# A transformer encoder layer on one core: TensorE's order in the attention written out, with filler in six portions per unit, and residual steps, norm sums, first wave and tail rearranged

## The chip, the cores and the metric

The kernel runs on one core of a Trainium2 chip. A core has five engines with a queue each, all in order: TensorE (PE, matrix products and transposes), VectorE (DVE), ScalarE (ACT), GpSimd (POOL) and SyncE (SP, which here issues the DMAs). An instruction waits in its queue until what it needs is done, and what stands behind it waits too. The metric is the time of one execution in microseconds (us); less is better.

## The reference

One layer over 2048 tokens with 1024 features, all in float32. `mod` holds six vectors made from the conditioning input `c`:

```
mod = silu(c) @ ada_w + ada_b                 # sh1, sc1, g1, sh2, sc2, g2
h = rmsnorm(x, mix_norm_pre) * (1 + sc1) + sh1
q, k, v = split(h @ w_qkv)                    # 16 query heads of 64, 4 key/value heads
logits = q k^T / 8 + bias                     # blocks of 128 queries against 3 x 128 keys
p = softmax([logits, sink])[..., :-1]         # |key - query| <= 128
y = (p v) @ w_o
x = x + g1 * rmsnorm(y, mix_norm_post)
h = rmsnorm(x, ffn_norm_pre) * (1 + sc2) + sh2
y = (silu(a) * b) @ w_out,  a, b = split(h @ w_in)   # 2816 hidden features
x = x + g2 * rmsnorm(y, ffn_norm_post)
```

## The kernel before, in words

Tokens lie in four chunks of 512 columns, features in tiles of 128 partitions. A float32 matrix is split into a high part (rounded, `act.copy`, ScalarE) and a low part (the rest, a subtraction on VectorE or GpSimd); `three` (line 147) multiplies hi x hi, hi x lo and lo x hi, three matmuls of 512 columns. A norm's sum over features is a matmul with ones (`rstd_of`, line 118), as a rule with the sum of squares split in the same way (lines 128 to 132), then a logarithm, an exponential and one Newton step (lines 136 to 141).

Stages, by their place in the profiled execution:

- 0 to 23.5 us: load and norm of chunk 0. 23.5 to 74: the first wave, seven of the twelve q/k/v tiles of chunk 0, with the feature tile k as the outer loop, so that each of eight steps needs one more weight piece (split by ScalarE and GpSimd) and two reductions of the modulation (`ada_reduce`, 128x1024, VectorE).
- to 177: the rest of chunk 0 and chunk 1. `evac` (line 208) splits a finished tile into a buffer `e` (two buffers) and writes it to DRAM (`q_d`, `k_d`, `v_d`).
- 177 to 750: attention in 64 units, one for a chunk c, a group g of four heads with one key/value head, and a query block jb. `scores` (line 421) makes for each of the four heads two matmuls, a VectorE step that adds the bias and finds the maximum (line 437), and an exponential on ScalarE; then a reciprocal and four normalisations on GpSimd (line 445). `values` (line 448), two units later (`LAG`), has for each of three key blocks four transposes, a split of the result (`phi` on ScalarE, `plo` on VectorE) and two products into `o`, then two additions and a DMA to `o_d`. Between the units stands filler: in the first 32 units q/k/v of chunks 2 and 3 (`psq`, 576 matmuls), in the last 32 the output projection of chunks 0 to 2 (`py`, 576 matmuls), whose inputs `ol` are loaded from `o_d` and split, and whose weights `wor` are loaded, split into `wo`, and kept in `wo_d`. A finished projection chunk has steps at its end (`ends`, line 586): norm, residual (three GpSimd operations a tile, lines 507 to 515), norm, `h2`.
- 750 to 821: the projection of chunk 3 (GpSimd's split goes to VectorE there). To 2085: the feed-forward network by a seven-product scheme for 2x2 blocks. To 2164: its last part and the end of the layer; the norms of chunks 2 and 3 (`lo`, `l`) lie inside the feed-forward part.

The program order is written unit by unit (line 652), `fill.pull` giving 18 or 20 filler matmuls after each. A scheduler then orders the instructions of each engine by its own costs and priorities, so the order on an engine is not the program's. `tc.issue_after` holds an instruction until another is placed. SP has one queue, in which loads and writes of all stages stand in turn.

Of the kernel before, what the change touches and what calls it, by code (L numbers as in the profile page):

```python
# [11 lines left out]
F32 = mybir.dt.float32  # L12
# [34 lines left out]
FILL = (18, 20)  # L47
# [7 lines left out]

HOLD = 6
# [17 lines left out]
def encoder_layer(ctx, tc, a):  # L74
    nc = tc.nc
    out = a["out"]
    act, dve, pool, pe, sp = nc.scalar, nc.vector, nc.gpsimd, nc.tensor, nc.sync

# [39 lines left out]
    def rstd_of(alloc, psp, ptag, acc, tag, r=None, direct=False):  # L118
# [5 lines left out]
        if direct or len(sums) > 1:  # L124
            for i, sq in enumerate(sums):
                pe.matmul(ps, f(ones), sq, start=i == 0, stop=i == len(sums) - 1)
        else:
            hi, lo = alloc(f"nhi{tag}")[:, :n].bitcast(F32R), alloc(f"nlo{tag}")[:, :n].bitcast(F32R)
            dve.tensor_copy(hi, acc)
            dve.tensor_tensor(lo, acc, f(hi), ALU.subtract)  # L130
            pe.matmul(ps, ones, hi, start=True, stop=False)
            pe.matmul(ps, ones, lo, start=False, stop=True)
# [7 lines left out]
        dve.tensor_scalar(t, t, -0.5, 1.5, ALU.mult, ALU.add)  # L140
        dve.tensor_tensor(r, r, t, ALU.mult)
# [5 lines left out]
    def three(ps, w, h, first=False, last=False):  # L147

        pe.matmul(ps, w[0], h[0], start=first, stop=False)  # L149
        pe.matmul(ps, w[0], h[1], start=False, stop=False)  # L150
        pe.matmul(ps, w[1], h[0], start=False, stop=last)  # L151
# [55 lines left out]

    def evac(c, n, ps, psp, ptag):

        t = ev.tile([P, 2, CH], F32R, tag="e", name=f"e{c}_{n}")  # L210
# [30 lines left out]
    with ExitStack() as pa:  # L241
        w2 = open_pool(pa, "w2", side="right")
        raws = open_pool(pa, "raws", 5, side="right")
        w1 = open_pool(pa, "w1", side="right")
        psA = open_pool(pa, "psA", 8, space=PSUM)
# [5 lines left out]
        sp.dma_start(gains, a["gains"])  # L251
        act.activation(cb, cb, AF.Silu)
# [3 lines left out]
        def ada_load(t, pl):  # L256
            w = pl.tile([P, D], F32, tag="raw", name=f"ada{t}")
            sp.dma_start(w, a["ada_w"][t])
            return t, w
# [6 lines left out]
        def w_piece(k, i):  # L266
# [3 lines left out]
            t = pl.tile([P, 2, n], F32R, name=f"w{i}_{k}")  # L270
# [21 lines left out]
        for n in NORD[:WAVE]:  # L292
            evac(0, n, pss[n], psA, "mm")
# [3 lines left out]
        ch1.squares()  # L297
# [835 lines left out]
```

## Time and profile before

| what | us |
|---|---|
| runs | 2163.07, 2168.15, 2168.44 (median 2168.15) |
| the profiled execution | 2166.07, of which the span 2164.3 |
| first wave | 23.5 to 74 |
| attention, first half | 184 to 464 |
| attention, second half | 464 to 750 |
| projection of chunk 3 begins | 750 |
| feed-forward | 821 to 2085 |

The page gives busy time of each engine over the span. The view by windows gives the same for stretches, with the mean granted clock of TensorE (PEclk, 1.00 is full speed). The waits tell what an engine's idle time ended with: "s L432 <- DVE nm L437" is a score that waited until a VectorE step of line 437 had freed its buffer. In a timeline a row has start, length, engine, line, operation, out<-in and count; brackets hold the idle time before it and what released it.

### The profile page before, as it was taken

The numbers are of one execution on the slowest core, as the hardware profiler recorded it, in microseconds if no ns is written. First come the engines' busy times: TensorE is split into PE (matmuls) and PEld (weight loads), VectorE is DVE, ScalarE is ACT, GpSimd is POOL, SyncE is SP. The second block draws the span as 40 slices with busy tenths as digits, with TensorE's granted clock in tenths as the row PEclk, the third lists the DMA queues.
The fourth block names the chain that finished last, engine by engine and source line by source line (L and its number), as shares of the span: only waits on it lengthen the run. The fifth ranks groups of instructions, "written<-read, shape, count | busy, mean of one in ns | idle before, by whom it ended". The sixth has DMA issues, their size and how long they took to land. (4 is left out here: it accounts for less than half of the span.)

```text
span 2164.3 us, 28995 instructions
## 1 busy us (share of the span) xinstructions
PE 2055.8 (95%) x9366; PEld 1666.6 (77%) x9366; DVE 1649.8 (76%) x2933; ACT 1076.4 (50%) x2125; POOL 737.5 (34%) x687
## 2 busy tenths in 40 slices
PE   6898999989989989999999999999999999998996
PEld 4786877878867768878887877888888788877886
DVE  7656767665676669876878897767673888999987
ACT  4546666577777746343434342333332844465422
POOL 3404343367778723434344422222221000220030
PEclk8999999999999989999999999999999999999998
DMA  8877665576667695545455764332231644438442
GB/s 279 261 254 253 184 182 175 159 282 233 227 199 245 189 347 206 183 148 162 138 178 194 257 220 142 112 106 94 98 117 54 210 153 138 141 129 280 161 132 103
DMA packets 200516, 396.35 MB, mean 183 GB/s; under 512 B 20091, under 2 KB 62124, under 8 KB 195244
## 3 DMA queue, kind: packets, MB, share of 16 engines
q1 hardware_dynamic: 199788, 393.97, 54.7%
q8 instruction: 74, 1.21, 0.2%
q14 instruction: 78, 0.64, 0.1%
q10 hardware_dynamic: 576, 0.52, 0.1%
HBM read 270.65 MB, written 123.76 MB: 182 GB/s over the span
## 5 line engine op out<-in xcount | busy, mean ns | idle before, releaser
L437 DVE CUSTOM_DVE_ANT_0 pr<-s,bias,nsink 128x384 f32<-128x384 f32 (+1 forms) x256 | 149.3, 596 | 91.5 <-PE s L432 74.3
L149 PE MATMUL pc_i<-ht,ws_i 128*128 128x512 f32 x528 | 207.2, 393 | 2.1 <-DVE b_i L799 1.5
L150 PE MATMUL pc_i<-ht,ws_i 128*128 128x512 f32 x528 | 206.9, 392 | 0.0
L151 PE MATMUL pc_i<-ht,ws_i 128*128 128x512 f32 x528 | 206.9, 392 | 0.0
L439 ACT ACTIVATE pr<-pr,nm 128x385 f32<-128x385 f32 (+1 forms) x256 | 153.8, 603 | 71.3 <-DVE nm L437 64.3
L815 POOL TENSOR_TENSOR p_i<-p_i,u_i 128x512 f32<-128x512 f32 x44 | 71.5, 1625 | 310.7 <-DVE u_i L802 153.6
L445 POOL TENSOR_SCALAR pr<-pr,rs 128x384 f32<-128x384 f32 (+1 forms) x256 | 147.4, 601 | 83.0 <-DVE rs L443 82.9
L946 POOL TENSOR_TENSOR z<-z,z 128x512 f32<-128x512 f32 x32 | 52.5, 1654 | 359.2 <-DVE z L942 342.3
L432 PE MATMUL s<-k,q 128*128 128x384 f32 (+1 forms) x512 | 136.1, 359 | 20.2 <-DVE nm L437 13.6
L149 PE MATMUL pc_i<-hb,wa_i 128*128 128x512 f32 x352 | 139.1, 395 | 2.0 <-DVE u_i L789 2.0
L150 PE MATMUL pc_i<-hb,wa_i 128*128 128x512 f32 x352 | 138.7, 394 | 0.0
L151 PE MATMUL pc_i<-hb,wa_i 128*128 128x512 f32 x352 | 138.7, 394 | 0.0
L155 DVE TENSOR_TENSOR plo<-t,phi 128x512 fp32r<-128x512 f32 x184 | 121.7, 685 | 16.2 <-ACT phi L154 14.7
L154 ACT CAST wa_i<-wiri 128x512 fp32r<-128x512 f32 x132 | 81.8, 620 | 102.2 <-PE pc_i L151 94.7
L154 ACT CAST ws_i<-s_i 128x512 fp32r<-128x512 f32 x132 | 81.6, 618 | 102.5 <-PE pc_i L151 98.7
L432 PEld LDWEIGHTS s<-k,q 128*128 128x128 f32 x512 | 86.6, 193 | 44.9 <-DVE nm L437 27.8
L149 PEld LDWEIGHTS pc_i<-ht,ws_i 128*128 128x128 f32 x528 | 99.3, 188 | 25.5 <-DVE b_i L799 2.2
L151 PEld LDWEIGHTS pc_i<-ht,ws_i 128*128 128x128 f32 x528 | 99.2, 188 | 22.4
L150 PEld LDWEIGHTS pc_i<-ht,ws_i 128*128 128x128 f32 x528 | 99.2, 188 | 22.2
L455 PE MATMUL t<-ident,pr 128*128 128x128 f32 x736 | 113.1, 273 | 3.1 <-POOL pr L445 2.4
L149 PE MATMUL py<-ol,wo 128*128 128x512 f32 x256 | 103.3, 405 | 11.9 <-ACT wo L154 7.4
L155 DVE TENSOR_TENSOR ws_i<-s_i,ws_i 128x512 fp32r<-128x512 f32 x132 | 104.6, 792 | 10.9 <-ACT ws_i L154 10.7
(320 smaller groups left out, 6142.8 us busy)
## 6 DMA issues: line engine op xcount, KB each, us to landing
wiri<-w_in SPq DMA_DIRECT2D x88, 512.0 KB, 4.8
ada<-ada_w SPq DMA_DIRECT2D x40, 512.0 KB, 4.9
wiro<-w_out SPq DMA_DIRECT2D x48, 384.0 KB, 3.9
q_d<-e SPq DMA_DIRECT2D x64, 256.0 KB, 3.9
q<-q_d SPq DMA_DIRECT2D x16, 1024.0 KB, 5.8
wo<-wo_d SPq DMA_DIRECT2D x16, 1024.0 KB, 5.7
g_d_b<-p_i SPq DMA_DIRECT2D x44, 256.0 KB, 4.7
g_d_t<-p_i SPq DMA_DIRECT2D x40, 256.0 KB, 2.0
```

The source lines that it names most:

```text
L149: pe.matmul(ps, w[0], h[0], start=first, stop=False)
L150: pe.matmul(ps, w[0], h[1], start=False, stop=False)
L151: pe.matmul(ps, w[1], h[0], start=False, stop=last)
L154: act.copy(hi, src)
L155: return eng.tensor_tensor(lo, src, f(hi), ALU.subtract).ins
L432: m = pe.matmul(ps[:, :n], q[:, h, jb * P:(jb + 1) * P], kk[:, i, (jb + j0) * P:(jb + j1) * P], start=i == 0, stop=i == 1)
L437: red = dve.tensor_tensor_reduce(pr[:, h, :n], ps[:, :n], bias[g][:, h, j0 * P:j1 * P], -1.0, nsink[:, hh:hh + 1], ALU.add, ALU.min, nm[:, ...
L439: act.activation(pr[:, h, :n + 1], pr[:, h, :n + 1], AF.Exp, bias=nm[:, h:h + 1], scale=-1.0, accum_out=rs[:, h:h + 1])
L445: pool.tensor_scalar(pr[:, h, :n], pr[:, h, :n], rs[:, h:h + 1], 1.0, ALU.mult, ALU.mult)
L455: pe.transpose(pt[:, h * P:(h + 1) * P], pr[:, h, jj * P:(jj + 1) * P], ident)
L815: pool.tensor_tensor(sa, sa, b, ALU.mult)
L946: (pool if (i, x) in ((2, 2), (4, 4), (5, 5), (6, 6)) else dve).tensor_tensor(sums[hf, n2, x], sums[hf, n2, x], sums[hf, n2, y], ALU.add)
```

## The change

1. `FILL` becomes a table with one number per unit; the matmuls of scores, transposes, products and filler are stamped (`inorder`), so TensorE takes them in program order. `scores` and `values` become generators, and a unit is written as: two scores, filler, transposes, one score, filler, transposes, one score, filler, product, transposes, filler, product, filler, product, filler, each filler a sixth of the unit's number.
2. The steps at a projection chunk's end are taken one per unit (`end_step`), two residual tiles each, by turns all on GpSimd and all on VectorE, with two sums; `HOLD` goes; every third weight tile of the projection comes into two separate halves; 66 filler matmuls remain after the last product, where 53 did.
3. Norm sums are no longer split. In the feed-forward part the sums of `lo` and `l` are issued a step later. The Newton step loses an instruction: its factor -0.5 goes into `gains`, on GpSimd.
4. In the first wave the first eight modulation tiles are loaded into the buffers of the second weight part, `evac` has a third buffer (`eva`) for every third tile, and the squares of chunk 1 come after the wave's last evacuation, on VectorE.
5. q, k, v and bias of unit 0 are loaded with high priority, `x` of chunk 3 after them. In the tail, `finish` of the last chunk's first half is spread over n = 4 to 7.

```diff
-FILL = (18, 20)
+FILL = [0, 4, 12, 16] + 16 * [20] + 12 * [19] + [4, 8, 12] + 21 * [17] + 8 * [12]
...
+    def inorder(m):
+        tc.stamp_issue_order_token(m.ins, "attention")
+        return m
...
-        if direct or len(sums) > 1:
-            for i, sq in enumerate(sums):
-                pe.matmul(ps, f(ones), sq, start=i == 0, stop=i == len(sums) - 1)
-        else:
-            hi, lo = alloc(f"nhi{tag}")[:, :n].bitcast(F32R), alloc(f"nlo{tag}")[:, :n].bitcast(F32R)
-            dve.tensor_copy(hi, acc)
-            dve.tensor_tensor(lo, acc, f(hi), ALU.subtract)
-            pe.matmul(ps, ones, hi, start=True, stop=False)
-            pe.matmul(ps, ones, lo, start=False, stop=True)
+        for i, sq in enumerate(sums):
+            pe.matmul(ps, f(ones), sq, start=i == 0, stop=i == len(sums) - 1)
...
-        dve.tensor_scalar(t, t, -0.5, 1.5, ALU.mult, ALU.add)
-        dve.tensor_tensor(r, r, t, ALU.mult)
+        dve.scalar_tensor_tensor(r, t, -3.0, r, ALU.add, ALU.mult)
...
-        t = ev.tile([P, 2, CH], F32R, tag="e", name=f"e{c}_{n}")
+        ev_, nev[0] = (eva if nev[0] % 3 == 2 and c < 2 else ev), nev[0] + 1
+        t = ev_.tile([P, 2, CH], F32R, tag="e", name=f"e{c}_{n}")
...
+        pool.tensor_scalar(gains, gains, -0.5, 1.0, ALU.mult, ALU.mult)
...
-                ada_reduce(*ada_load(8 + k, raws))
-                ada_reduce(*ada_load(k, raws))
+                for t in (8 + k, k):
+                    ada_reduce(*ada_load(t, w2 if k < KT // 2 else raws))
...
-        ch1.squares()
+        with tc.issue_after(ins):
+            ch1.squares((dve, dve))
...
-                dve.tensor_scalar(nsink, nsink, -1.0, None, ALU.mult)
+                pool.tensor_scalar(nsink, nsink, -1.0, 1.0, ALU.mult, ALU.mult)
...
-    def residual(c, k, y, xr, r, acc, alloc, eng=dve):
+    def residual(c, k, y, xr, r, acc, engs=(pool, dve, pool), first=True):
         sp.dma_start(xr, a["xT"][c, :, k, :])
-        pool.tensor_tensor(y, y, r, ALU.mult)
-        eng.tensor_tensor(y, y, xr, ALU.add)
+        engs[0].tensor_tensor(y, y, r, ALU.mult)
+        engs[1].tensor_tensor(y, y, xr, ALU.add)
...
             for k in range(KT):
-                residual(c, k, self.ys[k], yp.tile([P, CH], F32, tag="xr", name=f"xr{c}_{k}", bufs=3), r,
-                         self.acc, rot(yp, "nsq", 4), pool)
-                if k % 4 == 3:
+                residual(c, k, self.ys[k], yp.tile([P, CH], F32, tag="xr", name=f"xr{c}_{k}", bufs=4), r,
+                         accs[k % 2], [(pool, dve)[k % 2]] * 3, False)
+                if k % 2 and k < KT - 1:
                     yield
+            dve.tensor_tensor(accs[0], accs[0], accs[1], ALU.add)
...
+    def end_step():
+        while ending and next(ending[0], ending) is ending:
+            del ending[0]
...
-    load_qkv(0, 0)
-    load_bias(0)
+    with tc.high_priority(offset=400):
+        load_bias(0)
+        first_load = load_qkv(0, 0)
...
-        un.scores()
+        sc = un.scores()
+        vl = units[i - LAG].values() if i >= LAG else iter(())
+        part = FILL[i] / 6
+        next(sc)
+        next(sc)
+        fill.pull(part)
+        next(vl, None)
+        next(sc)
+        fill.pull(part)
+        next(vl, None)
+        next(sc)
...
-        if i >= LAG:
-            units[i - LAG].values()
-            done = i - LAG + 1
-        fill.pull(FILL[i >= half])
+        fill.pull(part)
+        next(vl, None)
+        next(vl, None)
+        fill.pull(part)
+        next(vl, None)
+        fill.pull(part)
+        next(vl, None)
+        done = max(i - LAG + 1, 0)
+        fill.pull(part)
+        end_step()
     for un in units[-LAG:]:
-        un.values()
+        for _ in un.values():
+            fill.pull(3)
+        end_step()
...
             acc = temp(f"lacco{c}")
             sp.dma_start(acc, acc_d[c - CPH])
+            yield
             rstd_of(temp, psF, "mm", acc, f"lo{c}", r)
-            yield
```

How the order moves, at three places. First TensorE in the second half of attention (`s` scores, `t` transposes, `o` products, `py` filler). Before, in a stretch without filler:

```order
L432 MATMUL s_0_2_6774<-k_0_6198,q_0_6196 128x384 x2
L432 MATMUL s_0_3_6779<-k_0_6198,q_0_6196 128x384 x2
L432 MATMUL s_0_0_6851<-k_0_6198,q_0_6196 128x384 x2
L432 MATMUL s_0_1_6856<-k_0_6198,q_0_6196 128x384 x2
L460 MATMUL o_3_6685<-phi_3_0_6691,v_3_5777 128x512
L461 MATMUL o_3_6685<-plo_3_0_6692,v_3_5777 128x512
L460 MATMUL o_3_6685<-phi_3_1_6702,v_3_5777 128x512
L455 MATMUL t_3_0_6790<-ident,pr_3_6544 128x128 x4
L461 MATMUL o_3_6685<-plo_3_1_6703,v_3_5777 128x512
L460 MATMUL o_3_6685<-phi_3_2_6713,v_3_5777 128x512
L455 MATMUL t_3_1_6801<-ident,pr_3_6544 128x128 x4
L461 MATMUL o_3_6685<-plo_3_2_6714,v_3_5777 128x512
```

Four scores of two units stand behind each other here; elsewhere twenty to twenty-five filler matmuls do. After, in the same half:

```order
L437 MATMUL s_2_0_5959<-k_2_5322,q_2_5320 128x384 x2
L437 MATMUL s_2_1_5964<-k_2_5322,q_2_5320 128x384 x2
L144 MATMUL py_6_5881<-ol_3_4929,wo_6_5874 128x512
L145 MATMUL py_6_5881<-ol_3_4929,wo_6_5874 128x512
L146 MATMUL py_6_5881<-ol_3_4929,wo_6_5874 128x512
L461 MATMUL t_2_0_5972<-ident,pr_2_5771 128x128 x4
L437 MATMUL s_2_2_5981<-k_2_5322,q_2_5320 128x384 x2
L144 MATMUL py_6_5881<-ol_3_4929,wo_6_5874 128x512
L145 MATMUL py_6_5881<-ol_3_4929,wo_6_5874 128x512
L146 MATMUL py_6_5881<-ol_3_4929,wo_6_5874 128x512
L461 MATMUL t_2_1_5989<-ident,pr_2_5771 128x128 x4
L437 MATMUL s_2_3_5998<-k_2_5322,q_2_5320 128x384 x2
```

Three filler matmuls now stand between the parts of a unit.

Second, VectorE after the first wave (`e` evacuations in the order 8, 9, 0 to 4; `nacc` the sum of squares of chunk 1, `nhia`, `nloa` its split, `nr` the norm's factor). Before:

```order
L182 TENSOR_TENSOR nacc_862<-nacc_862,nsq_7_882 128x512
L155 TENSOR_TENSOR e_8_767<-psq_8_448,e_8_767 128x512
L129 CAST nhia_1007<-nacc_862 128x512
L155 TENSOR_TENSOR e_9_774<-psq_9_449,e_9_774 128x512
L130 TENSOR_TENSOR nloa_1008<-nacc_862,nhia_1007 128x512
L216 SCALAR_TENSOR_TENSOR e_0_781<-psq_0_450,e_0_781 128x4x128
L139 SCALAR_TENSOR_TENSOR nta_1013<-nsta_1006,nta_1013 128x512
L140 TENSOR_SCALAR nta_1013<-nta_1013 128x512
L141 TENSOR_TENSOR nr_1005<-nr_1005,nta_1013 128x512
L216 SCALAR_TENSOR_TENSOR e_1_786<-psq_1_451,e_1_786 128x4x128
```

The sum of chunk 1 is complete before the first evacuation. After:

```order
L214 SCALAR_TENSOR_TENSOR e_0_784<-psq_0_453,e_0_784 128x4x128
L214 SCALAR_TENSOR_TENSOR e_1_789<-psq_1_454,e_1_789 128x4x128
L214 SCALAR_TENSOR_TENSOR e_2_794<-psq_2_455,e_2_794 128x4x128
L214 SCALAR_TENSOR_TENSOR e_3_799<-psq_3_456,e_3_799 128x4x128
L214 SCALAR_TENSOR_TENSOR e_4_804<-psq_4_457,e_4_804 128x4x128
L177 TENSOR_TENSOR nacc_865<-nacc_865,nsq_1_867 128x512
L177 TENSOR_TENSOR nacc_865<-nacc_865,nsq_2_870 128x512
L177 TENSOR_TENSOR nacc_865<-nacc_865,nsq_3_873 128x512
L177 TENSOR_TENSOR nacc_865<-nacc_865,nsq_4_876 128x512
```

All seven additions now stand behind the last evacuation of the wave. On TensorE the sum of these squares (`nsta`) stands, after the change, ahead of the tiles 5, 6 and 7 of chunk 0; before it stood between the two v tiles of chunk 0.

Third, SP at the middle of attention (`ol` the loads for the first projection; `q_1`, `k_1` the loads for the units after the next four; `wor`, `o_d`, `q_d` other DMAs). Before:

```order
L553 DMA wor_2_5222<-w_o 128x1024
L469 DMA o_d_3_115<-of_3_4783 256x1x128
L543 DMA ol_0_4996<-o_d_0_108 128x1024
L543 DMA ol_1_5000<-o_d_1_109 128x1024
L397 DMA q_1_4946<-q_d_1_69 128x2048
L401 DMA k_1_4948<-k_d_1_81 128x2x128
```

After:

```order
L495 DMA o_d_3_115<-of_3_4793 256x1x128
L583 DMA wor_2_5336<-w_o 128x1024
L401 DMA q_1_4978<-q_d_1_69 128x2048
L405 DMA k_1_4980<-k_d_1_81 128x2x128
L407 DMA k_1_4980<-k_d_1_85 128x2x512
L410 DMA k_1_4980<-k_d_1_89 128x2x128
L570 DMA ol_0_4917<-o_d_0_108 128x1024
L570 DMA ol_1_4921<-o_d_1_109 128x1024
```

The loads of q and k for the later units stand ahead of the first `ol` now; the buffer that this q goes into is freed by the last score of unit 31.

More of the change, by code (lines that the diff above doesn't have):

```diff
@@ L553, in fill @@
                     sp.dma_start(raw, a["w_o"][n])
[L554 to L558 removed]
+                    split(*w, raw, dve if c else pool)
+                if c < NCH - 1:
+                    for i in range(2):
+                        d = (f(w[i]), wo_d[n][:, i])
+                        sp.dma_start(*(d if c else d[::-1]))
                 ps = psF.tile([P, CH], F32, tag="mm", name=f"py{c}_{n}")
```

148 lines of the change are left out of this document (84 added, 64 removed).

## The prediction

> **What bounds the kernel now.** I read the page first, then the view by windows (length; busy time and, in brackets, instructions of PE, PEld, DVE, ACT and POOL; then PEclk, DMA share and GB/s), then the waits of PE and the timelines at the places where it waits.
>
> ```profile
> span 2164.3 us, 28995 instructions
> ...
> PE 2055.8 (95%) x9366; PEld 1666.6 (77%) x9366; DVE 1649.8 (76%) x2933; ACT 1076.4 (50%) x2125; POOL 737.5 (34%) x687
> ```
>
> ```profile
> 23.50:74.00 50.50, 45.69 (x171) 35.64 (x172) 43.79 (x53) 24.86 (x37) 28.53 (x14) 0.87 0.75 253
> 84.00:87.50 3.50, 3.49 (x9) 2.72 (x10) 2.29 (x4) 1.05 (x2) 0.00 (x0) 0.53 0.91 257
> 177.00:184.00 7.00, 0.76 (x4) 0.36 (x3) 0.69 (x1) 0.60 (x1) 0.54 (x3) 0.70 0.94 322
> 184.00:464.00 280.00, 268.68 (x1377) 221.82 (x1377) 197.73 (x509) 183.04 (x433) 112.75 (x167) 0.99 0.62 187
> 464.00:480.00 16.00, 13.09 (x66) 10.35 (x65) 10.19 (x29) 14.40 (x31) 13.18 (x14) 1.00 1.03 397
> 464.00:750.00 286.00, 270.93 (x1372) 216.55 (x1370) 185.24 (x479) 218.16 (x494) 222.83 (x259) 1.00 0.67 227
> 592.00:627.00 35.00, 29.01 (x155) 20.68 (x153) 26.66 (x77) 30.59 (x79) 35.00 (x50) 1.00 0.65 215
> 750.00:778.00 28.00, 16.98 (x56) 12.56 (x57) 14.86 (x15) 11.82 (x15) 9.07 (x7) 0.80 1.03 376
> ```
>
> TensorE sets the end, so only time in which it issues nothing can be won. In attention the busy column hides part of that, since a matmul's record is longer than the step from one start to the next. I take the steps from a dense piece of the timeline.
>
> ```profile
> 454.83 0.52 PE L432 MATMUL s<-k,q 128*128 128x384 f32 x2
> 455.19 1.47 PE L455 MATMUL t<-ident,pr 128*128 128x128 f32 x12
> 456.42 0.48 PE L149 MATMUL psq<-hi,ws 128*128 128x512 f32 x1
> 456.73 0.39 PE L150 MATMUL psq<-lo,ws 128*128 128x512 f32 x1
> 456.96 0.39 PE L151 MATMUL psq<-hi,ws 128*128 128x512 f32 x1
> ```
>
> So a score matmul costs 0.18 us (0.36 for two), a transpose 0.103 (1.23 for twelve), a 512-wide one 0.23. The first half of attention (184 to 464) holds 576 filler matmuls, 172 products, 257 scores and 370 transposes: 134 + 40 + 44 (those of block 0 are narrower) + 38, with the norm 257 us of 280. The second (464 to 750) holds 529, 196, 256 and 383: 123 + 46 + 46 + 39 + 2 for norms, 256 of 286. Some 23 and 30 us are lost there, 53 together; at 592 to 627 POOL is busy for all 35 us.
>
> **The change, part by part.** The sum is made against the profiled execution, 2166.07 us (1.8 around the span); the median of the runs is 2.1 above it.
>
> *First wave and the norm of chunk 1.* VectorE is the fullest engine behind PE in the wave, 43.8 of 50.5 us. These are groups of 23.5 to 74, then the same kind of split on VectorE over the whole kernel:
>
> ```profile
> L155 DVE TENSOR_TENSOR lo<-x,hi 128x512 fp32r<-128x512 f32 x8 | 10.6, 1320 | 0.7 <-ACT hi L154 0.7
> ...
> L182 DVE TENSOR_TENSOR nacc<-nacc,nsq 128x512 f32<-128x512 f32 x4 | 4.5, 1114 | 6.0 <-POOL nacc L182 4.3 <-ACT nsq L181 1.7
> L358 DVE TENSOR_SCALAR nsink<-nsink 128x16 f32<-128x16 f32 x1 | 2.1, 2056 | 0.0
> ```
>
> ```profile
> L155 DVE TENSOR_TENSOR plo<-t,phi 128x512 fp32r<-128x512 f32 x184 | 121.7, 685 | 16.2 <-ACT phi L154 14.7
> ```
>
> The change takes the nacc additions (4.5 us) and nsink (2.1) out of the wave, and lets eight modulation tiles load without waiting for a raw buffer. I take 4 us earlier of the 6.6 (bounds 0 and 9, the upper one with the raw waits).
>
> The lo split costs 1320 ns here and 685 elsewhere, and POOL is busy beside it. The Trainium skill (GPSIMD Engine Reference, Specifications) says that GpSimd shares its SBUF interfaces with VectorE and contends with VectorE instructions that have two SBUF inputs; the trace agrees, 1320 against 685 ns. By that rule removing POOL's additions would also shorten what stays, by an estimate of a third of 8 x 0.64, and the wave would gain 5.7 us; by the rows of removed work alone 4.
>
> What is given back: chunk 1's additions now stand behind the last evacuation of the wave (e_4), and PE's sum nsta stands ahead of the three remaining q tiles of chunk 0, so those and all of chunk 1 wait for it.
>
> ```profile
> 75.64 7.47 SPq L225 DMA_DIRECT2D k_d<-e  x8
> ...
> 85.34 0.63 SPq L220 DMA_DIRECT2D q_d<-e  x1
> ```
>
> ```profile
> 82.63 0.60 ACT L215 ACTIVATE e<-psq 128x512 fp32r<-128x512 f32 x1 [2.67 <-DMA k_d<-e]
> ```
>
> ```profile
> 84.01 0.64 PE L149 MATMUL psq<-hi,w 128*128 128x512 f32 x1 [2.62 <-DVE e L216]
> ...
> 97.41 0.39 PE L149 MATMUL psq<-hi,w 128*128 128x512 f32 x1
> ```
>
> The third buffer takes e_0 at once, but e_1 now has the place that e_0 had, waiting for the k writes until 82.6; its two q writes leave by 85.7, behind e_0's, and land 3.9 us later by
>
> ```profile
> q_d<-e SPq DMA_DIRECT2D x64, 256.0 KB, 3.9
> ```
>
> So e_4, which needs that buffer, starts at 89.6 and is out at 91; seven additions at 0.685 end at 95.8. The sum is no longer split:
>
> ```profile
> 2125.07 1.02 PE L126 MATMUL nstz<-zacc,ones 128*128 128x512 f32 x2
> 2125.53 0.68 PE L149 MATMUL pl<-gls,wl 128*128 128x256 f32 x1
> 2126.05 0.28 PE L150 MATMUL pl<-gls,wl 128*128 128x256 f32 x1
> ```
>
> 0.98 less one 256-wide step of 0.12 is 0.86. That gives 96.7, or 92.7 after the 4 us. Then psq_5: 24 x 0.23 = 5.6, plus 1.6 because PE restarts slowly (clock 0.53 for 3.5 us in the window at 84). End 99.9, where before it was 97.4. Net **+3** (bounds -3: e_4 earlier; +8: no gain in the wave).
>
> *Start of attention.* PE works 0.76 of the 7 us from 177 to 184, waiting for k. q and k now load earlier, but the four bias loads move behind the q writes of e_3, around 175, and weights behind these. The first softmax step before is at
>
> ```profile
> 184.54 0.48 DVE L437 CUSTOM_DVE_ANT_0 pr<-s,bias,nsink 128x256 f32<-128x256 f32 x1 [5.68 <-PE s L432]
> ```
>
> A bias landing 7 to 9 us after 175 replaces one wait by another: **0** (-3 to +3).
>
> *Order in attention.* The work is the same; the lost time per unit is now 53 / 64 = 0.83 us, bunched between runs of bare units and bursts of filler. Even portions give each of the four scores, three transposes and products 0.7 us of filler as cover. First half: of 23 I leave 11, **-12** (0 to -18). Second half without 464 to 480: of 27 I leave 13, **-14** (0 to -22). There residual steps go half to VectorE: 24 operations at POOL's
>
> ```profile
> L507 POOL TENSOR_TENSOR y<-y,no 128x512 f32<-128x512 f32 x16 | 20.1, 1296 | 0.7 <-DVE no L141 0.7
> ```
>
> 1.3 us leave POOL (31 us of 223) and cost VectorE 24 x 0.685 to 24 x 1.114, 16 to 27 us. ACT then is the fullest helper, 218 us of some 270. Should ACT or VectorE fall behind its place, the fixed order has nothing else for PE.
>
> *Unit 32.* The first projection matmul stands after two scores of unit 32; its load stands on SP behind q and k of a later group, which wait for unit 31's last score.
>
> ```profile
> 460.65 1.24 SPq L543 DMA_DIRECT2D ol<-o_d  x2
> ```
>
> ```profile
> 469.49 0.73 PE L149 MATMUL py<-ol,wo 128*128 128x512 f32 x2 [0.32 <-ACT ol L154]
> ```
>
> ```profile
> 469.91 4.76 POOL L155 TENSOR_TENSOR ol<-ol 128x1024 fp32r<-128x1024 f32 x2
> ```
>
> From issue to first use it is 8.8 us before, and 2.4 more for POOL's low half. With some 3 us for the issues ahead, the second matmul can go 14 us after unit 31's last score; PE gets there after about 6. That is 8 us idle and a slow restart of 1.6, against 2.9 idle in the window 464 to 480 before, 6.7 more. Behind that matmul stand the other scores and the transposes of two units, so VectorE and ScalarE run dry too. Filler is thin there by the table (4, 8, 12 for units 32 to 34), and POOL may come to the split sooner: **+5** (0 to +8).
>
> *Seam.* The waits of PE in 745 to 780:
>
> ```profile
> PE py L149 <- ACT wo L154: 7.4, 1, 7.4
> PE py L149 <- DMA wo<-wo_d: 3.6, 1, 3.6
> ```
>
> After the last product 66 filler matmuls remain, 15.2 us, over the output's write, load and split, and the loads stand earlier on SP. **-11** (-3 to -14; if loads still come late only the 3.6 goes).
>
> *Norm sums and the FFN.* Each unsplit sum costs 0.86 - 0.46 = 0.40 us of PE. Seven lie in attention: **+2.8**. Four in the FFN cost 1.6; there the sum stood behind a VectorE cast:
>
> ```profile
> 942.83 0.79 PE L131 MATMUL nstl<-nhil,ones 128*128 128x512 f32 x1 [4.05 <-DVE nhil L129]
> ```
>
> 4.05 and the slow restart 1.6, with 1.4 for the second such sum, go if it is issued a step later without a cast: 1.6 - 7 = -5.4, taken as **-4.5** (-6 to 0).
>
> *At nothing.* The factor -0.5 in gains and nsink's sign on POOL, behind the start's loads; the weights of the projection in two tiles, the same bytes in two DMAs, whose issues SP has room for between units. If SP had none, its queue would show at unit 32, which is priced.
>
> *Tail.* Three small VectorE steps less, the additions stay in their order: **-0.5** (-2 to 0).
>
> Sum: 3 + 0 - 12 - 14 + 5 - 11 + 2.8 - 4.5 - 0.5 = -31.2, that is 2134.9; with part of the 2.1 to the median, **2136**.
>
> **Rivals.**
> *Everything is covered.* The steady parts come near to the dense piece of the timeline, 5 us left in each half, and the loads arrive: -1 - 18 - 22 + 1 - 14 + 2.8 - 7 - 1.5 = -59.7, **2106**. For it: no engine beside PE is over 78% in 464 to 750. Against it: the order says that a load stands behind a late score.
>
> *The fixed order makes PE wait.* A softmax step or a normalisation queued behind a residual or a modulation sum delays a score, and PE has no filler ahead. Place: every unit. Price: 1.2 us a unit in place of 0.83, 77 us for 64 units against 50 now outside 464 to 480, +27; the other terms make -5. **2188**, slower. It decides from 50 + 5 = 55 us, 0.86 a unit. For it: POOL 35.00 of 35, DMA at 1.03 in 464 to 480, and VectorE steps of 1.1 us beside POOL. Against it: two units of lag between scores and products.
>
> *The order was not the cost.* The losses follow POOL, loads and buffers, so the steady parts stay, the seam gives 6: 3 + 5 - 6 + 2.8 - 4.5 - 0.5 = 0, **2166**. For it: 592 to 627. Against it: the first half loses 23 with POOL at 40%.
>
> **How the numbers follow.** The forecast 0.52, all covered 0.20, waiting 0.12, not the cost 0.16. The forecast's own range is 2110 to 2160. For 8 in 10 I take 2098 to 2172: the first rival is inside, the third too, the slower one is left out. A difference under 0.3%, 6.5 us, can't be told from none. Faster: 0.51 + 0.20 + 0.04 = 0.75; same 0.11 from the third and the forecast's edge; slower 0.14.
>
> **What would show it.** Right: PE without waits over 1 us from 215 to 455; an idle of about 10 us with a slow clock at 82 to 93, and of 8 us at unit 32; no wait on wo at the seam; none on nstl. Wrong: scores waiting for nm in most units, a new wait for bias or weights over 5 us, or POOL still full for tens of us in the second half.

## The result: slower, 2245.0 us against 2168.1, and the profile after

The changed kernel's runs are 2233.62, 2244.49, 2245.52 and 2249.40 us, median 2245.0; those of the kernel before beside it 2163.07 to 2168.44, median 2168.1. The ratio is 1.0348 [1.0328, 1.0368]: 77 us slower, where 31 us faster were forecast, and outside the range (2098 to 2172).

Busy time by engine, from the page of the changed kernel (its span is 2242.7 us):

```profile
PE 2083.7 (93%) x9366; PEld 1680.9 (75%) x9366; DVE 1660.7 (74%) x2920; ACT 1080.5 (48%) x2126; POOL 702.4 (31%) x662
```

The work is the same: 9366 matmuls as before, VectorE's busy time 11 us longer, GpSimd's 35 us shorter. So the time is idle time of TensorE, and the slower clock behind it. The view by windows, cut at the first score, the first score of unit 32, the first projection matmul of chunk 3 and (by count of matmuls) late in the feed-forward part, tells where; first the kernel before:

```profile
0.00:183.74 183.74, 150.13 (x684) 120.35 (x685) 118.26 (x179) 86.21 (x145) 47.22 (x34) 0.92 0.80 264
183.74:463.79 280.05, 268.73 (x1377) 221.87 (x1377) 197.73 (x509) 183.04 (x433) 112.75 (x167) 0.99 0.62 187
463.79:774.15 310.36, 284.31 (x1421) 226.72 (x1419) 196.43 (x492) 227.88 (x506) 231.91 (x265) 0.99 0.70 239
774.15:1688.22 914.07, 904.13 (x3897) 734.45 (x3897) 705.72 (x999) 349.52 (x591) 290.27 (x188) 0.99 0.46 159
1688.22:2164.30 476.08, 448.46 (x1993) 363.19 (x1991) 431.66 (x756) 229.76 (x451) 55.39 (x34) 0.97 0.48 160
```

and the changed kernel:

```profile
0.00:179.66 179.66, 149.99 (x684) 120.12 (x685) 107.77 (x171) 86.22 (x144) 44.16 (x31) 0.92 0.78 262
179.66:500.84 321.18, 282.84 (x1368) 228.71 (x1366) 202.25 (x510) 185.50 (x437) 110.73 (x172) 0.94 0.56 170
500.84:844.94 344.10, 298.59 (x1430) 237.32 (x1428) 223.90 (x510) 229.36 (x503) 207.23 (x238) 0.94 0.64 220
844.94:1767.75 922.81, 904.92 (x3897) 733.43 (x3896) 699.17 (x981) 349.94 (x593) 283.88 (x189) 0.99 0.45 155
1767.75:2242.70 474.95, 447.35 (x1993) 361.29 (x1991) 427.65 (x751) 229.50 (x451) 56.40 (x34) 0.98 0.49 161
```

The stages differ by -4.1, +41.1, +33.7, +8.7 and -1.1 us, together the 78.4 of the spans. Nearly all of it is attention, both halves. The +8.7 belongs to the cut: before, PE's waits at the change to chunk 3 (7.4 and 3.6 us, shown with the prediction) lay ahead of it, after (8.3 and 0.7) they lie behind it. Without these waits on either side the second half is some 45 us longer, and the stage behind it as long as before. In both halves the granted clock fell from 0.99 to 0.94: the gaps cost twice, once as idle time and once as slow matmuls behind them. 0.06 of 321 us less 0.01 of 280 is up to 16 us in the first half, and in the second by the same working up to 18.

Before, PE waited 11 us in the first half and 25 in the second, 11 of these at the change to chunk 3. The largest kind beside those 11 was this, in the first half and then in the second (us in total, times, longest):

```profile
PE s L432 <- DVE nm L437: 5.0, 8, 2.0
...
PE s L432 <- DVE nm L437: 8.6, 14, 1.6
```

What PE waited for in the first half of the changed kernel, its five largest:

```profile
PE o L472 <- DVE plo L150: 8.5, 11, 4.4
PE psq L144 <- ACT ws L149: 8.2, 3, 5.9
PE o L471 <- ACT phi L149: 7.1, 8, 2.4
PE s L437 <- DVE nm L440: 6.7, 3, 5.6
PE psq L146 <- POOL ws L150: 5.9, 3, 2.8
```

and in the second half, its four largest:

```profile
PE o L472 <- DVE plo L150: 16.1, 20, 5.0
PE s L437 <- DVE nm L440: 13.9, 10, 6.7
PE py L144 <- ACT ol L149: 7.2, 1, 7.2
PE o L471 <- ACT phi L149: 5.2, 7, 1.9
```

These kinds are 36 us in 28 waits and 42 in 38. That is about one wait for each unit, but they are not the even small waits of the slower rival: of all 71 in the two halves, 83 us together, the 20 of at least 1 us make 62 us, and single ones take 4 to 7. Two of the places look like this; those at the start and at the edges of the stages stand with the points of the prediction below.

**A late weight, in the first half.** Filler weights `wsr` and the modulation tiles `ada` share one set of buffers. A timeline of VectorE, SP, ScalarE and PE:

```profile
416.65 1.28 DVE L265 CUSTOM_DVE_ANT_0 ada<-ada,cb,adab 128x1024 f32<-128x1024 f32 x1
417.96 0.67 SPq L512 DMA_DIRECT2D wsr<-w_qkv  x1
423.39 1.04 ACT L149 CAST ws<-wsr 128x1024 fp32r<-128x1024 f32 x1 [2.37 <-DMA wsr<-w_qkv]
424.34 0.58 ACT L149 CAST phi<-t 128x512 fp32r<-128x512 f32 x1
424.97 0.50 PE L471 MATMUL o<-phi,v 128*128 128x512 f32 x1 [2.36 <-ACT phi L149]
```

The weight is asked for as the reduction of a modulation tile ends. ScalarE stands 2.37 us idle at its split, with `phi`, whose input is long there, queued behind it; PE stands 2.36 us at the product that needs `phi`. In a fixed order a late weight so stops a product that does not use it, and PE, which has other matmuls to do (the filler that follows at 426 us uses the weight before), may not do them.

**VectorE busy with a run of its own, in the second half.** The program gives one residual step per unit, with one multiplication on VectorE. But only TensorE's order is fixed: on VectorE the scheduler has put the four multiplications of a chunk in a row, beside four on GpSimd:

```profile
635.62 6.33 POOL L535 TENSOR_TENSOR y<-y,no 128x512 f32<-128x512 f32 x4 [1.75 <-DVE no L136]
636.05 6.45 DVE L535 TENSOR_TENSOR y<-y,no 128x512 f32<-128x512 f32 x4
...
643.69 0.79 PE L472 MATMUL o<-plo,v 128*128 128x512 f32 x1 [4.96 <-DVE plo L150]
```

PE idles 4.96 us for the `plo` behind them. Over the half, by groups:

```profile
L535 POOL TENSOR_TENSOR y<-y,no 128x512 f32<-128x512 f32 x8 | 12.7, 1611 | 2.5 <-DVE no L136 2.5
L535 DVE TENSOR_TENSOR y<-y,no 128x512 f32<-128x512 f32 x8 | 12.3, 1601 | 0.0
```

1.60 us each on VectorE, where the prediction had 0.685 to 1.114 for every operation of these steps.

### The profile page after: what moved, and what is told of

Its sections match the earlier page's. It is cut to its first block, busy times and chain, and to the rows that moved or that the text cites. A ratio compares the mean times of both kernels' runs of the same rounds, so it can differ in the third digit from the quotient of the medians.

```text
span 2242.7 us, 28970 instructions
## 1 busy us (share of the span) xinstructions
PE 2083.7 (93%) x9366; PEld 1680.9 (75%) x9366; DVE 1660.7 (74%) x2920; ACT 1080.5 (48%) x2126; POOL 702.4 (31%) x662
## 5 line engine op out<-in xcount | busy, mean ns | idle before, releaser
L150 DVE TENSOR_TENSOR plo<-t,phi 128x512 fp32r<-128x512 f32 x184 | 126.5, 688 | 60.9 <-ACT phi L149 59.1
L150 DVE TENSOR_TENSOR ws_i<-s_i,ws_i 128x512 fp32r<-128x512 f32 x132 | 110.1, 834 | 14.1 <-ACT ws_i L149 13.9
L149 ACT CAST phi<-t 128x512 fp32r<-128x512 f32 x184 | 106.7, 580 | 23.0 <-PE t L461 21.9
L150 DVE TENSOR_TENSOR wa_i<-wiri,wa_i 128x512 fp32r<-128x512 f32 x132 | 105.7, 802 | 15.7 <-ACT wa_i L149 15.4
```

Source lines behind the costliest of these rows:

```text
L149: act.copy(hi, src)
L150: return eng.tensor_tensor(lo, src, f(hi), ALU.subtract).ins
```

## The experiments

In the tables "first half" runs from the first score to that of unit 32, "second half" from there to the first projection matmul of chunk 3, both of the profiled execution. Before: 280 and 310; after: 321 and 344.

### The order alone: taken away, and added alone

e1_free is the changed kernel without the stamp, so that the scheduler orders TensorE again:

```diff
     def inorder(m):
-        tc.stamp_issue_order_token(m.ins, "attention")
         return m
```

> The changed kernel with the stamp taken off the attention's matmuls, all else kept (portions, residual by turns, loads, norms). Theory A: the fixed order of TensorE turns each late input into a stall; a scheduler's order lets filler pass, so the waits of TensorE between 177 us and the end of attention fall from 92 us to under 45 and the time to 2150 to 2185 us. Rival B: the moved loads and the residual steps on VectorE cost the time whatever TensorE's order is: then it stays at 2225 us or more.

e2_fixed is the kernel before with the stamp, the generators, the six portions and the table, and nothing else of the change.

> The kernel before with only the stamped order, the portions and the table of numbers; loads, residual on GpSimd, split norm sums, first wave and tail as before. Theory A: the fixed order alone costs, 2205 us or more. Rival B: the fixed order alone is harmless or a gain, 2175 us or less, and the loss is in the other edits.

| run | median us | ratio to before | first half | second half |
|---|---|---|---|---|
| after | 2245.0 | 1.0348 [1.0328, 1.0368] | 321 | 344 |
| e1_free | 2192.0 | 1.0108 [1.0086, 1.0130] | 285 | 330 |
| e2_fixed | 2240.9 | 1.0324 [1.0299, 1.0350] | 316 | 343 |

One line taken away gives back 53 of the 77 us (2192.0 is 7 above the range of the theory, and 33 below the rival's bound), and the order added alone costs 72. The halves of e2_fixed are those of its fastest run, 2229.9 us. So the order by itself makes the kernel slower. In the first half it is nearly all of the loss (285 against 280). The second half of e1_free is still 20 us longer than before, so something else of the change costs time there. The costs do not add up (72 for the order, 24 for the rest, 77 together): they are partly the same waits.

### The residual steps on VectorE

e3_pool is the changed kernel, e5_free_pool is e1_free, each with all residual steps on GpSimd, one per unit as the change has them:

```diff
-                         accs[k % 2], [(pool, dve)[k % 2]] * 3, False)
+                         accs[k % 2], [pool] * 3, False)
```

> The changed kernel with all residual operations on GpSimd. Theory C: runs of four multiplications on VectorE (5.9 to 6.5 us at 636 and 749 us) ahead of a score's or a split's step cost some 20 us with the slow clock behind them: 2220 to 2230 us, and the waits of 5.0 and 6.7 us go. Rival D: GpSimd is then the late engine, with its normalisations behind residual operations, and the time stays within 8 us of 2245 or rises.

> The changed kernel without the stamp and with all residual operations on GpSimd. Theory C: with a free order the runs on VectorE still cost what the second half lost against the kernel before (some 20 us of the 24 that remain): 2165 to 2178 us. Rival D: GpSimd's load is what the second half then waits for, as in the kernel before and worse: 2185 us or more.

| run | median us | ratio to before | first half | second half |
|---|---|---|---|---|
| e3_pool | 2217.7 | 1.0233 [1.0216, 1.0250] | 322 | 325 |
| e5_free_pool | 2168.4 | 1.0002 [0.9991, 1.0013] | 286 | 304 |

With the fixed order they cost 27 us, 19 of them in the second half (and the wait at the seam, 8.3 us in the changed kernel, is down to 2.2 in e3_pool). With the free order they cost 24, all in the second half. Without the stamp and with the steps on GpSimd the kernel is back at the time of before: these two edits hold the whole 77 us, and the gains and losses of all others cancel. The row of the second half of e1_free, then that of e5_free_pool:

```profile
464.78:794.82 330.04, 296.74 (x1456) 240.01 (x1454) 238.82 (x549) 243.11 (x536) 212.55 (x242) 0.95 0.73 256
```

```profile
466.20:770.01 303.81, 279.09 (x1432) 228.00 (x1430) 190.43 (x492) 227.16 (x508) 227.77 (x264) 0.99 0.74 249
```

In the shorter stretch VectorE works 48 us less, GpSimd 15 us more, and the clock is back at 0.99. 27.7 us of the 48 are the residual steps; most of the rest is work for the next stages that falls into the longer stretch. GpSimd was the fullest of the helpers before (232 of 310 us), but PE waited for it only 1.5 us in that half; VectorE, with 63%, makes `nm` and `plo`, which PE needs in every unit.

e4_spread left the steps on VectorE, and held each until the first softmax step of its unit was placed (`red`; `sink` does the same on GpSimd); it also took the norm steps of chunk 3 one at a time:

```diff
-        end_step()
+        end_step(un.red, un.sink)
...
-            if i < 2:
-                for k in range(4 * i, 4 * i + 4):
-                    ch3.h(k)
+                if i == 1:
+                    with tc.issue_after(now[0].red):
+                        ch3.h(k)
```

> The changed kernel with the steps at a projection chunk's end, and chunk 3's normalisation, held on VectorE and GpSimd behind the current unit's first score step, so that their multiplications no longer stand in runs. Theory C: stalls at 204 to 222 us and at 636 to 816 us go, 25 to 40 us: 2205 to 2220 us. Rival D: the fullness of VectorE and GpSimd and not the runs is the cause: within 8 us of 2245.

2230.8 us, 1.0290 [1.0275, 1.0305], halves of 319 and 330: a gain of 14 us, all in the second half but for 2. That is neither the 25 to 40 us of the theory nor the rival's 8 at most. At 635 us two multiplications stand in a row now (3.10 us) where four did: parting the run wins half of what moving it to the other engine wins.

### The parts of the change that are not in attention's order

e6_free_pool_sq is e5_free_pool with `ch1.squares()` back inside the wave; e9_best is that with the split norm sums, their places and the Newton step of the kernel before. e7_norms is the norm edit alone on the kernel before, e8_wave the wave's edit alone (modulation tiles in the second weight part's buffers, third buffer for `evac`, sign of nsink on GpSimd; squares where they were).

```diff
# e6_free_pool_sq
-        with tc.issue_after(ins):
-            ch1.squares((dve, dve))
+        ch1.squares()
```

> As the run before (no stamp, residual on GpSimd), and the squares of chunk 1 again inside the first wave, on GpSimd and VectorE. Theory E: the sum behind the last evacuation makes TensorE idle 10 us at 80 to 91 us; undone, the wave ends some 3 us later and the kernel gains 3 to 8 us on the run before. Rival: the work only moves back into the wave, whose VectorE is full, and the time stays within 3 us.

> The kernel before with the norm edit alone: sums unsplit, the Newton step one instruction shorter, the sums of the feed-forward norms a step later. Prediction's terms: +2.8 in attention and -4.5 in the feed-forward part, so 2162 to 2168 us and no wait on a norm's cast at 943 us. Rival: the longer sums stand in the way and another wait takes the place of the cast: 2170 us or more.

> The kernel before with the first eight modulation tiles in the second weight part's buffers, the third evacuation buffer and nsink's sign on GpSimd, and chunk 1's squares left in the wave. Theory: 4 us (0 to 9) at the wave's end that reach the end of the kernel: 2159 to 2168, best 2164. Rival: attention's start waits for k anyway, so that nothing arrives: within 2 us of 2168.

> No stamp, residual on GpSimd, chunk 1's squares in the wave (2159.2 us), and the norm sums split again with the sums of the feed-forward norms in their old place. The norm edit alone cost 0.17% on the kernel before; if costs add, this is 3 to 5 us under 2159.2: 2154 to 2157. Rival: the norm edit is a gain where the sum no longer stands alone; then 2160 or more.

| run | median us | ratio to before |
|---|---|---|
| e6_free_pool_sq | 2159.2 | 0.9959 [0.9944, 0.9973] |
| e7_norms | 2172.8 | 1.0017 [1.0008, 1.0026] |
| e8_wave | 2162.6 | 0.9976 [0.9966, 0.9987] |
| e9_best | 2148.2 | 0.9913 [0.9894, 0.9932] |

The squares behind the last evacuation cost 9 us (2168.4 to 2159.2; the first score comes at 170.72 us in place of 180.31), the norm edit 11 in this kernel (2159.2 to 2148.2) and 4 on the kernel before; the wave's edit alone gains 5 to 6. Left in e9_best are the wave's edit, the loads of unit 0, the ends one step per unit, the weight tiles in halves, the tail and the even portions without the stamp: 0.9913, faster than before. Why the norm edit costs more than its 2.8 us of PE stayed open. In e7_norms the first half takes 288 us in place of 280, with few norm sums in it, so the scheduler's order has changed there too; that is a reading, not shown.

### Which inputs are late under the fixed order

e11_table changes the table alone, with no filler for units 0 to 2, 31 and 32. e10_repaired is that with the residual on GpSimd, the squares in the wave and chunk 3's norm steps spread.

```diff
-FILL = [0, 4, 12, 16] + 16 * [20] + 12 * [19] + [4, 8, 12] + 21 * [17] + 8 * [12]
+FILL = [0, 0, 0, 12] + 27 * [21] + [0] + [0, 12, 12] + 21 * [17] + 8 * [12]
```

> The changed kernel with only the table's numbers altered: no filler in units 0 to 2, 31 and 32, 21 in units 4 to 30. Theory: the waits for the first weights (5.9 us) and for the first projection input (7.2 and 1.6) go with their slow clock, 15 to 20 us: 2225 to 2230. Rival: units without filler lose as much by waiting for their own softmax: within 8 us of 2245.

> The stamped order kept, with the late inputs found so far taken out: no filler in units 0 to 2, 31 and 32 (so the first filler matmul of each half comes a unit or more later), residual on GpSimd, chunk 1's squares in the wave, chunk 3's normalisation spread over eight steps. Theory A: a fixed order costs only through late inputs; with these named ones gone it comes to 2165 to 2190 us. Rival: other inputs are late in their place, or units without filler wait for their own steps; then 2195 us or more.

e11_table took 2237.2 us, 1.0313 [1.0297, 1.0328] (320 and 337), e10_repaired 2200.5, 1.0152 [1.0133, 1.0172] (319 and 319). With less filler at the start, the waits up to 222 us fell from 19 to 13 (e11_table) and 14 us (e10_repaired), but those behind it grew from 19 to 27 and 25, and the first half stayed as long as it was. So the theory that the long waits at the start and VectorE's runs were the loss of the first half fell, and e10_repaired stayed above the 2165 to 2190 that went with it. The largest waits of e10_repaired from 222 us on:

```profile
PE psq L146 <- POOL ws L150: 6.9, 3, 2.7
PE o L470 <- ACT phi L149: 6.7, 7, 2.1
PE psq L144 <- ACT ws L149: 5.4, 3, 3.2
```

They are the weights and, behind their split on ScalarE, `phi`: the place read at 416 us above.

e13_adabuf gives attention's modulation tiles a buffer of their own (in the room of the fourth `ptp` buffer); e12_noada leaves out those 15 loads and reductions, so that 15 of the 48 columns of `mod` hold their bias alone.

```diff
# e13_adabuf
-                w = pl.tile([P, D], F32, tag="raw", name=f"ada{t}")
+                w = pl.tile([P, D], F32, tag="raw" if pl is raws else "ada", name=f"ada{t}", bufs=None if pl is raws else 1)
...
-    ptp = open_pool(att, "ptp", 4, side="right")
+    ptp = open_pool(att, "ptp", 3, side="right")
# e12_noada
-            waiting = [ada_load(late.pop(0), ws)] if late else []
+            waiting = []
```

> The changed kernel with the modulation tiles of the attention in a buffer of their own (and three in place of four buffers for the split transposes, to make room), so that a filler weight's load no longer waits for a reduction on VectorE. Theory G: in the first half TensorE waits because these loads are late, and because the weight's split stands ahead of a transposed block's split on ScalarE: the 14 us of waits on weights and some 8 of those on phi and plo go, the first half (321 us) falls to 295 to 305 and the time to 2220 to 2230. Rival H: other inputs are late in their place, as when the table was altered; the first half stays above 314 us and the time within 8 us of 2245.

> The changed kernel without the 15 loads and reductions of modulation tiles in the attention: 15 of the 48 columns of the modulation keep their bias alone, so this part of the computation is left out. Theory G: as in the run before, and VectorE is freed of 15 steps of 1.3 us: first half 290 to 302 us, 2212 to 2228. Rival H: first half above 314 us, time above 2235.

| run | median us | ratio to before | first half | second half |
|---|---|---|---|---|
| e13_adabuf | 2216.2 | 1.0213 [1.0194, 1.0231] | 295 | 342 |
| e12_noada | 2207.2 | 1.0167 [1.0148, 1.0186] | 291 | 338 |

One buffer is worth 29 us, 26 of them in the first half, nearly as much there as leaving the work out (30). These are all of PE's waits from 222 to 474 us in e13_adabuf:

```profile
PE pvt L229 <- ACT vt L226: 1.8, 3, 0.9
PE o L472 <- DVE plo L150: 1.4, 3, 0.7
PE o L471 <- ACT phi L149: 0.6, 1, 0.6
PE s L437 <- DVE nm L440: 0.3, 1, 0.3
```

How many matmuls (of all kinds together) each kernel gets through in the same 233 us in the middle of the first half, in this order before, after, e1_free, e13_adabuf:

```profile
222.00:455.00 233.00, 225.05 (x1157) 185.91 (x1156) 158.39 (x414) 146.26 (x352) 94.57 (x144) 1.00 0.60 178
```

```profile
222.00:455.00 233.00, 215.91 (x1059) 176.71 (x1060) 143.23 (x365) 129.36 (x310) 79.61 (x130) 0.96 0.54 164
```

```profile
222.00:455.00 233.00, 226.69 (x1159) 185.12 (x1159) 155.33 (x400) 140.30 (x333) 86.74 (x137) 1.00 0.60 182
```

```profile
222.00:455.00 233.00, 228.88 (x1183) 190.30 (x1182) 163.65 (x414) 144.50 (x349) 88.99 (x141) 0.99 0.61 185
```

1157 before, 1059 after, 1159 without the stamp, and 1183 with the stamp and a buffer for the modulation tiles. So even portions in a fixed order do run densely once their inputs are in time, 2% above before. That is the cover that the prediction counted on, and it is about 5 us (2% of 233), not 12. (The kinds of matmul are mixed alike: with the prediction's steps for each kind the gain is also 2%.)

### Everything repaired, with and without the order

e14_fixed_all is e10_repaired with e13_adabuf's buffers and the split norms. e15_best_ada is e9_best with the same buffers, without the stamp.

> The stamped order with all late inputs found so far taken out: table with no filler in units 0 to 2, 31 and 32, residual on GpSimd, chunk 1's squares in the wave, chunk 3's normalisation spread, split norm sums as before, and the modulation tiles of the attention in a buffer of their own. Theory A with G: the fixed order costs only by late inputs, so it comes to 2150 to 2168 us, first half 285 to 295 us. Rival: the bare units and the second half's helpers keep it above the kernel before, 2175 us or more.

> The best run so far (no stamp, residual on GpSimd, squares in the wave, split norm sums, 2148.2 us) with the modulation tiles of the attention in a buffer of their own. Theory G: with a free order the scheduler already passes late weights, its waits on them in the first half are under 3 us, so it gains 0 to 4 us: 2144 to 2149. Rival: the same 26 us as with the stamp would be seen; then under 2135.

| run | median us | ratio to before | first half | second half |
|---|---|---|---|---|
| e14_fixed_all | 2179.7 | 1.0054 [1.0033, 1.0075] | 295 | 320 |
| e15_best_ada | 2143.2 | 0.9887 [0.9871, 0.9902] | 277 | 295 |

The middle of the first half, e14_fixed_all and then e15_best_ada (214 us of it, since its half ends at 447 us):

```profile
222.00:455.00 233.00, 228.09 (x1182) 190.57 (x1182) 164.62 (x403) 146.14 (x347) 89.73 (x140) 1.00 0.63 186
```

```profile
222.00:436.00 214.00, 210.97 (x1090) 177.53 (x1089) 150.28 (x372) 133.00 (x317) 86.71 (x123) 0.99 0.65 199
```

5.07 and 5.09 matmuls a us: there the written order and the scheduler's are equal. At the edges they are not, so the theory that a fixed order costs by the named late inputs alone fell too (2179.7, where it had 2150 to 2168). From the first score to 222 us the fixed order gets through 162 matmuls in 51.20 us, the free one through 217 in 51.83:

```profile
170.80:222.00 51.20, 38.26 (x162) 29.13 (x160) 37.34 (x92) 34.35 (x79) 17.86 (x28) 0.83 0.68 211
```

```profile
170.17:222.00 51.83, 45.59 (x217) 36.72 (x216) 40.86 (x103) 38.73 (x92) 21.58 (x33) 0.90 0.77 229
```

That is 55 matmuls, some 11 us at 5.07 a us, of the 18 by which the first halves differ. The written order loses where inputs come irregularly, when the loads of the first units arrive, and it gains nothing elsewhere. How much of the 55 is the stamp's and how much the table's, which gives units 0 to 2 no filler, was not tried apart. e14_fixed_all differs from e15_best_ada by the stamp, the table and the spread norm steps of chunk 3, and these cost 36 us. The 24 of them in the second half lie in many small waits (the largest of a kind is `plo`, 8.0 us in 24 waits); which inputs are late there was not settled. e15_best_ada beats both kernels: 25 us below before, 102 below the change. The buffer's gain without the stamp, 5 us (2148.2 to 2143.2), is small beside the spread of e9_best's runs, 2144.9 to 2157.1.

## Why the prediction was wrong, point by point

**The step that failed** is "Order in attention": "First half: of 23 I leave 11, -12", and "Second half ... -14". It took the lost time for a matter of how evenly filler lies, and let even portions win half of it. Measured were 41.1 and 33.7 us more (some 45 in the second half without the waits at the seam). Two errors are in it. First, the size of the gain: with timely inputs the even portions win some 5 us in the first half, and the free scheduler is as dense (e14_fixed_all, e15_best_ada). Second, the cost: the sum had none for taking away the scheduler's choice, 53 to 72 us by e1_free and e2_fixed. The prediction knew the risk, "the fixed order has nothing else for PE", and gave it 12 in 100 as a rival with 27 us. That rival had the right sign and, in "no filler ahead", the right mechanism; the late inputs were others for the most part, `phi` and `plo` for the products and the weights for the filler, and `nm` for 13 scores. Its argument against itself, the two units of lag between scores and products, was the wrong one to weigh: lag covers softmax, but filler has a lag of its own, that of its weights, and the weights' split stands on ScalarE ahead of `phi`. The price, spread evenly over 64 units, was also wrong: the loss is in some 70 waits of very different length, the longest 7.2 us, and the slower clock behind them. The third rival, that the order was not the cost before, has support: with the order left free, residual steps one per unit and the other edits of e9_best bring the second half from 310 to 301 us, and a buffer (e15_best_ada) to 295. It is not shown, since e9_best also keeps the portions in its program order.

- *First wave and chunk 1, +3*: with the start's 0, +0.9 at the first softmax step (185.39 against 184.54). The first score comes 4.1 us earlier, but only to wait (next point). nsta, whose end was forecast at 92.7, began at 90.23, and the next matmul followed at 91.31:

```profile
90.23 2.08 PE L128 MATMUL nsta<-nacc,ones 128*128 128x512 f32 x2 [10.52 <-DVE nacc L177]
```

  The chain was right (10.52 us of idle PE; "about 10" was forecast), both sizes were somewhat small: the wave's edit alone brings the first score from 183.74 to 177.54 us (e8_wave), 6 us where I took 4, and moving the squares gives back 9 us of the whole kernel (e5_free_pool, e6_free_pool_sq) where I took 7. (The first score of e6_free_pool_sq, at 170.72, overstates the gain: its first softmax step is at 177.59, since the bias is late there too.)
- *Start of attention, 0*: right, and as argued: the wait for `k` is gone, the first softmax step waits 4.21 us for its bias, and the scores behind it 5.64. What was not priced stands behind: a filler matmul and a product wait 10 us more.

```profile
185.39 0.48 DVE L440 CUSTOM_DVE_ANT_0 pr<-s,bias,nsink 128x256 f32<-128x256 f32 x1 [4.21 <-DMA bias<-tab_d]
...
185.94 1.22 PE L437 MATMUL s<-k,q 128*128 128x256 f32 x4 [5.64 <-DVE nm L440]
194.84 0.80 PE L144 MATMUL psq<-hi,ws 128*128 128x512 f32 x1 [5.87 <-ACT ws L149]
...
204.14 4.08 DVE L196 TENSOR_TENSOR x<-x,nr 128x512 f32<-128x512 f32 x6
208.87 0.79 PE L472 MATMUL o<-plo,v 128*128 128x512 f32 x1 [4.39 <-DVE plo L150]
```

  The last is a run of six norm steps on VectorE ahead of `plo`, which I had not seen as a thing that products wait for.
- *Residual steps on VectorE, 16 to 27 us of its time*: named, and priced at nothing on the path; they cost 24 (free) to 27 us (fixed). The VectorE time itself came out at the upper bound: 27.4 us, in 22 operations (not 24), of which the multiplications took 1.60 each. What failed is that the sum gave this time no cost on the path.
- *Unit 32, +5*: right in place and size. 8 us idle and more for the low half were forecast:

```profile
508.92 0.79 PE L144 MATMUL py<-ol,wo 128*128 128x512 f32 x1 [7.23 <-ACT ol L149]
```

  The matmul behind it waits 1.64 us for GpSimd's low half.

- *Seam, -11*: wrong; a wait took the place of the one removed. The last group's `ol` load is issued late on SP, behind weight loads, and its split starts later still:

```profile
846.89 0.42 SPq L570 DMA_DIRECT2D ol<-o_d  x1
...
857.55 0.79 PE L144 MATMUL py<-ol,wo 128*128 128x512 f32 x1 [8.34 <-ACT ol L149]
```

  8.34 us and 0.71 behind it, where 7.4 and 3.6 stood before: 2 gained, less than the lower bound of 3, "if loads still come late". The longer cover was there, but only loads that are issued early are covered.
- *Norm sums +2.8, feed-forward -4.5*: the wait on nstl is gone as forecast, and another stands nearby, 3.45 us at 927.28 for a weight's split on ScalarE, which stands behind the logarithm and exponential of the norm `lo`. Together the edit costs 4 us by e7_norms where I had -1.7.
- *Tail, -0.5*: the last stage is 1.1 us shorter; right within its bounds.

Of the signs of being right, the idle of 10 us ahead of nsta and that of 8 at unit 32 came true, and the wait on nstl went; "PE without waits over 1 us from 215 to 455" did not: there are six, the longest 2.8. Of the signs of being wrong, "a new wait for bias or weights over 5 us" came true twice (5.64 behind a bias, 5.87); "scores waiting for nm in most units" did not (13 waits).

## What to carry to other kernels

An order written by hand for one engine is only as good as the arrival of each of its inputs: with it, a buffer of their own for the modulation tiles was worth 29 us, without it about 5, so count, before fixing an order, what each instruction's inputs wait for on the other queues, filler's weights too. Runs of several operations on the engine that feeds the bottleneck (four residual steps, six norm steps) are to be priced by the wait of what stands behind them, not by that engine's share of busy time; the fuller engine, for which TensorE hardly waited, was the better place for them. And where a change has many parts, try them apart: e9_best keeps those that win, 0.9913, and beside the others they could not be seen.

## What the runs showed of the hardware that was not expected

The clock can fall after a gap of 2 us. At 706.19 a product came after 1.94 us without a matmul, and this was the window behind it:

```profile
706.19 0.50 PE L471 MATMUL o<-phi,v 128*128 128x512 f32 x1 [1.94 <-ACT phi L149]
```

```profile
706.10:709.60 3.50, 3.18 (x8) 2.48 (x9) 1.53 (x3) 0.62 (x2) 2.15 (x4) 0.59 0.00 0
```

This gap of 2 us thus cost up to 1.4 us more (0.41 of 3.5). Behind one of 2.36 us (424.97) the clock was 0.77 over as long a window, behind one of 1.10 (736.55) it stayed at 1.00. The Trainium skill (TensorE: Matmul & The Clock Gate, Part 1: The HAM clock gate) puts the fall to half clock after an idle window of about 3.4 us; here it came after less, and the measurement decides.

VectorE and GpSimd slowed each other where both took two float32 inputs from SBUF: 1601 and 1611 ns for the multiplications that ran side by side, against 0.68 us for `x<-x,nr` on VectorE (4.08 for six, quoted above, with GpSimd all but idle) and 1296 ns for GpSimd's multiplications in the kernel before. The Trainium skill (SBUF — State Buffer, Summary: rules for kernel authors) says that where a VectorE instruction has two SBUF inputs while the GpSimd one reads SBUF, the second to issue blocks until the first has finished. By that, four pairs would take 4 x (0.68 + 1.296) = 7.9 us, an estimate; they took 6.45, so the contention is there, but a little milder.
